# Encoder trunk on one core: shorter GpSimd subtractions, rope casts and a square on other engines, and another order of the first sums

## The chip, the core and the metric

The kernel runs on one core of a Trainium2 chip. The core has a matrix engine (TensorE, PE in the profile; PEld is its loading of weights), three engines for elementwise work (VectorE or DVE, ScalarE or ACT, GpSimd or POOL), and a queue engine (SyncE or SP) from which nearly all transfers start. Each engine takes its instructions in a fixed order, and waits on semaphores for what the others give it. The metric is the time of one execution in microseconds, as the median of several runs. Before the change it is 1354.4 us, the median of three runs from 1353.18 to 1356.97.

## What is computed

Two layers over a sequence of 512 rows of width 1024. Each layer is an attention part and a gated conv-MLP, both scaled and shifted by a vector `c`:

```python
for l in range(DEPTH):
    mod = jax.nn.silu(c) @ w_ada[l] + b_ada[l]
    sh_a, sc_a, gt_a, sh_f, sc_f, gt_f = [m[:, None, :] for m in jnp.split(mod, 6, axis=-1)]
    h = rms_norm(x, g_attn[l]) * (1.0 + sc_a) + sh_a
    x = x + gt_a * hybrid_mixer(h, w_in[l], diff_lambda[l], diff_subln[l], na_rpb[l], w_out[l], l)
    h = rms_norm(x, g_ffn[l]) * (1.0 + sc_f) + sh_f
    x = x + gt_f * conv_glu_ffn(h, w_up[l], conv_w[l], conv_b[l], w_down[l])
return rms_norm(x, g_final)
```

The mixer projects `h` with `w_in` and has three kinds of heads: four differential heads (two softmaxes, the second subtracted with a factor, then a norm over each head), six heads with three dilated windows, and six with a 2-D neighbourhood. The first two kinds turn their queries and keys by rotary angles (rope). The heads' outputs are projected with `w_out`.

## The kernel before

All data lie transposed: eight tiles `x` of 128 features by 512 positions. Products are made from rounded parts: a float32 operand is split into `hi` (rounded to the format fp32r) and `lo` (what is left), and a product is three matmuls, hi by hi, lo by hi and hi by lo (`mm3`, lines 487 to 489; in `v_rows` lines 760 to 762; in `first_g0` line 567).

**Weights** come in 128-partition units in a fixed list `UNITS`: eight units of `w_in` for the first projection ("g0", 768 columns), those of the values ("vd", "vb", "vc"), of the later queries and keys ("b", "cq", "ck", 1024 columns), of the output projection ("o1" with 640 columns, "o2"), and of the MLP. `emit_raw` starts a unit's load on SP (line 333) into one of four buffers `raw` (the first eight units have their own, `graw`). `emit_split` (line 336) makes `hi` by a cast on ACT (line 355) and `lo` by one subtraction over the whole unit (line 357): on POOL for g0 of the first layer, b, cq, ck, vc, vb, o1 and o2 (`on_pool`), on DVE for the rest. There are three buffers for split weights in attention, so a unit is split when an earlier one has been used (`free_unit`).

**Adaptive sums.** `ada_step` (line 406) makes one column of the modulation: a multiply-and-sum over a 512 KB tile of `w_ada` on DVE (line 416, with a short read of the accumulator), for the scales also an instruction on ACT (line 424), and it starts the load of a later tile on SP (`ada_load`, line 403).

**Start.** `first_g0` (line 501) loads `x`, squares its eight tiles on ACT (line 510), adds five of the squares up on DVE (line 512), sums over partitions on PE (line 516), takes the mean on DVE (line 518) and its power on POOL (line 520), spreads it with PE (line 523), multiplies on DVE (line 528), and makes the hi and lo parts of `h` (lines 540 to 543). The first two adaptive sums follow the squares in program order: one scale column and one shift column.

**Attention.** `rope_pair` (line 657) turns one pair of query and key chunks: four products on DVE (lines 669, 670), and for each half a sum (line 676), the cast to `hi` on ACT (line 683) and the `lo` part (line 688); the sum and the `lo` part run on the engine `E`, which is DVE for the pair d0 and POOL for d1, b0, b1 and b2. The four results go to DRAM on SP (line 696), from where the stacked queries and keys come back. A step of the differential heads (`diff_step`, line 992) is: scores on PE (line 1001), a maximum on DVE (line 1003), an exponential on ACT (line 1011), a weighted difference on DVE (lines 1017 to 1019), four transposes on PE (line 909), their `hi` cast on ACT (line 913) and `lo` part on DVE (line 917), and the products with the values on PE (lines 930, 932). `diff_norm` (line 953) norms a pair of heads. Its lines 967 and 968 put together a variance of eight columns on DVE.

**What sets the order.** The program text gives each instruction its place by a counter (`Clock`: a stage of a chain runs some steps after the one before). The framework's planner then fixes the order on each engine ahead of time: among the instructions that are ready by its own estimate it takes the one that was written first, so a later one can overtake an earlier one that isn't ready. On the chip the order is fixed. `tc.issue_after(ins)` ties the instructions of its block that run on `ins`'s engine behind `ins`, and no others.

Of the kernel before, what the change touches and what calls it, by code (L numbers as in the profile page):

```python
# [12 lines left out]
F32 = mybir.dt.float32  # L13
F32R = mybir.dt.float32r
BF16 = mybir.dt.bfloat16
AF = mybir.ActivationFunctionType
ALU = mybir.AluOpType
# [10 lines left out]
EPS = 1e-6  # L28
# [148 lines left out]
def build(ctx, tc, a):  # L177
    nc = tc.nc
    V, A, G, PE, SY = nc.vector, nc.scalar, nc.gpsimd, nc.tensor, nc.sync
# [156 lines left out]
    def emit_split():  # L336
        i = wst["split"]
        l, u = divmod(i, NU)
        kind = UNITS[u][0][0]
        if slots["w"]:  # L340
            w, pool, bufs = "w", wp, W_BUFS
        elif slots["f"] and kind in NEAR:
            w, pool, bufs = "f", fpool["p"], F_BUFS
        else:
            return False
        slots[w] -= 1
        where[i] = w
        wst["split"] += 1
        while wst["raw"] <= i:
            emit_raw()  # L350
        r = raws.pop(i)
        n = r.shape[1]
        hi = pool.tile([128, n], F32R, tag=w + "hi", bufs=bufs, name=f"{w}hi{uid()}")
        lo = pool.tile([128, n], F32R, tag=w + "lo", bufs=bufs, name=f"{w}lo{uid()}")
        A.copy(hi, r)  # L355
        on_pool = (l == 0 and u < 8) or kind in ("b", "cq", "ck", "vc", "vb", "o1", "o2")
        (G if on_pool else V).tensor_tensor(out=lo, in0=r, in1=hi.bitcast(F32), op=ALU.subtract)  # L357
        splits[i] = (hi, lo)
        while wst["auto"] and wst["raw"] < min(TOT, i + RAW_AHEAD):
            emit_raw()  # L360
        return True
# [139 lines left out]
    def first_g0():  # L501
        fp = fpool["p"]
        for _ in range(5):
            ada_load()
            ada_load()
            emit_raw()
        sq = []
        for k in range(KD):
            sq.append(fp.tile([128, S], F32, tag="xt", bufs=8, name=f"xq{k}"))
            A.activation(out=sq[k], in_=x[k], func=AF.Square)  # L510
            if k in (2, 4, 5, 6, 7):
                V.tensor_tensor(out=sq[0], in0=sq[0], in1=sq[k], op=ALU.add)
        st = ps("s", (128, 4))
        todo = [(k, j) for k in (1, 3, 0) for j in range(4)]
        for i, (k, j) in enumerate(todo):
            PE.matmul(st[:, j:j + 1], sq[k][:, j * 128:j * 128 + 128], ones, start=(i == 0), stop=(i == len(todo) - 1))
        v = tmp((128, 4), tag="sm4", bufs=4)
        V.tensor_scalar(out=v, in0=st, scalar1=1.0 / D, scalar2=EPS, op0=ALU.mult, op1=ALU.add)
        r = tmp((128, 4), tag="sm4", bufs=4)
        G.tensor_tensor(out=r, in0=v, in1=mh[:, 0:4], op=ALU.pow)  # L520
        rb = ps("s")
        for j in range(4):
            PE.matmul(rb[:, j * 128:j * 128 + 128], r[:, j:j + 1].to_broadcast([128, 128]), ident, start=True, stop=True)
        xt, h = [], []

        def norm_x(k):
            xt.append(fp.tile([128, S], F32, tag="xt", bufs=8, name=f"xt{k}"))
            V.tensor_tensor(out=xt[k], in0=x[k], in1=rb, op=ALU.mult)

        def mk(k):  # L530
            if wst["raw"] < 8:
                emit_raw()
            t = xt[k]
            emit_split()
            if k >= 1:
                wst["auto"] = True
            sc, sh = gsc[0][:, k:k + 1], mods(0, 0)[:, k:k + 1]
            hi, lo = [wp.tile([128, S], F32R, tag="h", bufs=16, name=f"h{uid()}") for _ in range(2)]
            h.append((hi, lo))
            ins = A.activation(out=hi, in_=t, func=AF.Identity, scale=sc, bias=sh)  # L540
            t2 = tmp()
            A.activation(out=t2, in_=t, func=AF.Identity, scale=sc, bias=sh)
            G.tensor_tensor(out=lo, in0=t2, in1=hi.bitcast(F32), op=ALU.subtract)
            if k == 5:
                with tc.issue_after(ins.ins):
                    late_consts()

        ada_step()
        ada_step()
        norm_x(0)  # L550
        norm_x(1)
        mk(0)
        norm_x(2)
        norm_x(3)
        ada_step()
        ada_step()
        mk(1)
        for k in range(4, KD):
            norm_x(k)
        banks = yield  # L560
        us = {}

        def mms(k, cs):
            wh, wl = us[k]
            for w, m in ((wh, 0), (wl, 0), (wh, 1)):
                for c in cs:
                    PE.matmul(banks[c], w[:, c * 128:c * 128 + 128], h[k][m], start=(k == 0 and w is wh and m == 0),  # L567
                              stop=(k == KD - 1 and m == 1))

        for k in range(KD):  # L570
            if k + 2 < KD:
                ada_step()
                ada_step()
                mk(k + 2)
            us[k] = next_unit(("g0", k))
            if k == 0:
                mms(0, range(5))
            elif k == 1:
                mms(1, range(5))
                mms(0, (5,))  # L580
                mms(1, (5,))
                free_unit()
            else:
                mms(k, range(6))
            if k:
                free_unit()
            ck.step()
        cest.close()
        late["pt"] = ctx.enter_context(tc.tile_pool(name="ppt", bufs=1, space=PSUM))
        yield h  # L590
# [49 lines left out]
    def attention_phase(l, gen, fest):  # L640
# [16 lines left out]
        def rope_pair(name, px, py, tag, ti, eng=None):  # L657
            C, Sn = rope[:, 2 * ti, :], rope[:, 2 * ti + 1, :]
            nv = 4 if name[0] == "d" else 2
            dd = 64 // nv  # L660
            sd = dp.tile([2 * nv, 4 * dd, S], F32, name=f"scr{l}{name[0]}{name[1]}")
            scr[name] = sd
            E = eng or V
            ts, nat = {}, {}

            def part(i):
                def s0():
                    ts[i] = take("tmp"), take("tmp")
                    V.tensor_tensor(out=ts[i][0], in0=(px, py)[i], in1=C, op=ALU.mult)  # L669
                    V.tensor_tensor(out=ts[i][1], in0=(py, px)[i], in1=Sn, op=ALU.mult)  # L670
                    if i == 1:
                        give(tag[0])
                        give(tag[1])

                def s1():
                    E.tensor_tensor(out=ts[i][0], in0=ts[i][0], in1=ts[i][1],
                                    op=(ALU.subtract, ALU.add)[i])
                    give("tmp")

                def s2():  # L680
                    av["nat"] -= 2
                    hi = at([128, S], F32R, "nat", 8)
                    A.copy(hi, ts[i][0])
                    nat[i] = hi

                def s3():
                    lo = at([128, S], F32R, "nat", 8)
                    E.tensor_tensor(out=lo, in0=ts[i][0], in1=nat[i].bitcast(F32), op=ALU.subtract)
                    nat[2 + i] = lo
                    give("tmp")  # L690

                return (0, {"tmp": 2}, s0), (1, {}, s1), (1, {"nat": 2}, s2), (1, {}, s3)

            def s4():
                for c in range(4):
                    SY.dma_start(sd[:, c * dd:c * dd + dd], nat[c].bitcast(F32))
                av["nat"] += 4
                mark(2, ("scr", name))

            ck.chain(*part(0), hold=True)  # L700
            ck.chain(*part(1), (2, {}, s4), hold=True)
# [251 lines left out]
        def diff_norm(c):  # L953
# [7 lines left out]
            def s1():  # L961
                sq = box["sq"]
                st = take("pt", (128, 4, 2))
                for j in range(4):
                    PE.matmul(st[:, j], sq[:, j * 128:j * 128 + 128], blk, start=True, stop=True)
                v = tmp((128, 4, 2), tag="sm8", bufs=6)
                V.scalar_tensor_tensor(out=v, in0=dns[c], scalar=EPS, in1=dns[c], op0=ALU.mult, op1=ALU.mult)
                V.scalar_tensor_tensor(out=v, in0=st, scalar=1.0 / 64, in1=v, op0=ALU.mult, op1=ALU.add)
                give("pt")
                give("tmp")  # L970
                r = tmp((128, 8), tag="sm8", bufs=6)
                G.tensor_tensor(out=r, in0=v.rearrange("p a b -> p (a b)"), in1=mh, op=ALU.pow)
                box["r"] = r
# [405 lines left out]
    out = a["out"].rearrange("m p n -> p m n")  # L1379
# [62 lines left out]
```

## Time and profile before

| | us |
|---|---|
| median of 3 runs | 1354.4 |
| lowest and highest run | 1353.18, 1356.97 |
| the profiled execution | 1349.55 |
| its span, first to last instruction | 1347.8 |
| busy: PE, DVE, ACT, POOL | 1285.7, 849.0, 639.8, 240.0 |

The profile is one execution. Lines are those of the kernel file, a row names the engine, the operation, the tile it writes and those it reads, and busy times are in us. A wait is the idle time of an engine before an instruction, put down to what came last. A stretch is given in us from the start of the span. Layer 0 begins its attention near 58, its MLP near 313; layer 1 near 723 and 970.

### The profile page before, as it was taken

To read this page: it belongs to the slowest core of one execution; us is meant where nothing else is said; L and a number is where in the kernel's file an instruction comes from. 1 tells how busy PE (TensorE), PEld (TensorE's weight loads), DVE (VectorE), ACT (ScalarE), POOL (GpSimd) and SP (SyncE) were. 2 spreads that over 40 slices of the span, in tenths; PEclk is the share of its full clock that TensorE was granted. 3 is DMA by queue.
4 is the path that set the end of the run, shared out by engine and by line. 5 is a ranking of instruction groups with operands and counts; after the bars stand their busy time and mean duration, and the time that the engine had idled before them with its cause. 6 is when DMAs were issued, how large, how long until landed. Compare 5 with 4: busy or idle time off the path is not lost.

```text
span 1347.8 us, 18449 instructions
## 1 busy us (share of the span) xinstructions
PE 1285.7 (95%) x6836; PEld 1102.7 (82%) x6836; DVE 849.0 (63%) x1534; ACT 639.8 (47%) x1150; POOL 240.0 (18%) x163
## 2 busy tenths in 40 slices
PE   5988899899999999999999989999999999999997
PEld 4877698778988888888899868987898888888886
DVE  5659777788676566656674786576775434443443
ACT  4546688665533233323342667887554313331331
POOL 2644522133000000000124344212400000000002
PEclk9999999998999999999999999999999999999999
DMA  9676667853466656665524755472433332333211
GB/s 361 232 207 168 187 199 220 233 161 118 148 204 187 201 175 187 199 191 168 173 77 132 189 156 167 121 212 81 125 118 102 94 94 94 94 94 99 86 36 63
DMA packets 75001, 207.28 MB, mean 154 GB/s; under 512 B 8608, under 2 KB 12576, under 8 KB 74784
## 3 DMA queue, kind: packets, MB, share of 16 engines
q1 hardware_dynamic: 74048, 203.72, 50.4%
q10 hardware_dynamic: 864, 2.39, 0.5%
q8 instruction: 54, 0.88, 0.3%
q14 instruction: 35, 0.29, 0.1%
HBM read 180.91 MB, written 15.73 MB: 146 GB/s over the span
## 4 chain that ended last, share of the span: by engine, by line
PE 72%; DMA 9%; DVE 7%; POOL 4%; issue 4%; ACT 3%; SPq 1%; POOLq 0%; DVEq 0%; ACTq 0%
PE pr L489 9%; PE pr L488 9%; PE pr L487 9%; PE s L488 5%; PE s L487 5%; PE s L489 5%; PE pt L488 4%; PE pt L489 4%; PE pt L487 4%; PE o L488 2%; PE o L489 2%; PE o L487 2%; PE pt L909 2%; DMA raw<-w 1%; PE pr L567 1%
## 5 line engine op out<-in xcount | busy, mean ns | idle before, releaser
L355 ACT CAST whi<-raw 128x1024 fp32r<-128x1024 f32 (+2 forms) x136 | 128.1, 943 | 229.6 <-PE pr L489 78.2
L357 POOL TENSOR_TENSOR wlo<-raw,whi 128x768 fp32r<-128x768 f32 (+2 forms) x58 | 115.0, 1988 | 299.4 <-ACT whi L355 275.4
L448 POOL TENSOR_TENSOR tmp<-tmp,tmp 128x256 f32<-128x256 f32 (+1 forms) x38 | 37.0, 976 | 714.3 <-ACT tmp L446 713.5
L357 DVE TENSOR_TENSOR wlo<-raw,whi 128x1024 fp32r<-128x1024 f32 (+1 forms) x78 | 90.8, 1164 | 101.4 <-ACT whi L355 100.6
L416 DVE CUSTOM_DVE_ANT_0 tmp<-raw,cb,par 128x1024 bf16<-128x1024 f32 x80 | 109.4, 1368 | 52.7 <-DMA raw<-w_ada 52.3
L355 ACT CAST fhi<-raw 128x1024 fp32r<-128x1024 f32 (+1 forms) x76 | 74.6, 985 | 130.6 <-PE pr L489 52.8
L357 DVE TENSOR_TENSOR flo<-raw,fhi 128x1024 fp32r<-128x1024 f32 (+1 forms) x74 | 86.9, 1175 | 56.8 <-ACT fhi L355 56.0
L487 PE MATMUL pr<-h,whi 128*128 128x512 f32 (+1 forms) x300 | 113.2, 378 | 0.4 <-DVE tmp L669 0.4
L489 PE MATMUL pr<-h,whi 128*128 128x512 f32 (+1 forms) x300 | 111.5, 372 | 0.4 <-DVE h L483 0.4
L488 PE MATMUL pr<-h,wlo 128*128 128x512 f32 (+1 forms) x300 | 111.7, 372 | 0.0
L487 PE MATMUL pr<-h,fhi 128*128 128x512 f32 (+1 forms) x244 | 86.8, 358 | 0.1
L488 PE MATMUL pr<-h,flo 128*128 128x512 f32 (+1 forms) x244 | 86.5, 356 | 0.0
L489 PE MATMUL pr<-h,fhi 128*128 128x512 f32 (+1 forms) x244 | 85.8, 358 | 0.3 <-DVE h L483 0.3
L917 DVE TENSOR_TENSOR pl<-pt,ph 128x512 fp32r<-128x512 f32 x80 | 54.6, 685 | 18.0 <-ACT ph L913 17.7
L1267 ACT ACTIVATE tmp<-tmp 128x512 f32<-128x512 f32 x44 | 27.6, 631 | 77.7 <-DVE tmp L1262 77.7
L489 PEld LDWEIGHTS pr<-h,whi 128*128 128x128 f32 x300 | 56.7, 189 | 9.5 <-DVE h L483 0.6
L487 PEld LDWEIGHTS pr<-h,whi 128*128 128x128 f32 x300 | 56.8, 189 | 8.9 <-DVE tmp L669 0.7
L488 PEld LDWEIGHTS pr<-h,wlo 128*128 128x128 f32 x300 | 56.9, 190 | 8.7 <-POOL wlo L357 0.6
L913 ACT CAST ph<-pt 128x512 fp32r<-128x512 f32 x80 | 46.5, 582 | 26.2 <-PE pt L909 25.9
L1003 DVE TENSOR_REDUCE sm<-s 128x1 f32<-128x512 f32 x64 | 42.9, 681 | 25.3 <-PE s L1001 25.0
L909 PE MATMUL pt<-cst,tmp 128*128 128x128 f32 x320 | 48.7, 275 | 9.9 <-DVE tmp L1019 7.0
L909 PEld LDWEIGHTS pt<-cst,tmp 128*128 128x128 f32 x320 | 37.7, 140 | 19.8 <-issue 5.9
(287 smaller groups left out, 3704.9 us busy)
## 6 DMA issues: line engine op xcount, KB each, us to landing
raw<-w SPq DMA_DIRECT2D x132, 512.0 KB
raw<-w_ada SPq DMA_DIRECT2D x80, 512.0 KB
raw<-w SPq DMA_DIRECT2D x64, 384.0 KB
araw<-w_ada SPq DMA_DIRECT2D x16, 512.0 KB
raw<-w SPq DMA_DIRECT2D x16, 320.0 KB
graw<-w SPq DMA_DIRECT2D x8, 384.0 KB
scr0b<-nat SPq DMA_DIRECT2D x12, 256.0 KB
qs<-nat SPq DMA_DIRECT2D x24, 128.0 KB
```

The costliest lines, as they stand in the source:

```text
L355: A.copy(hi, r)
L357: (G if on_pool else V).tensor_tensor(out=lo, in0=r, in1=hi.bitcast(F32), op=ALU.subtract)
L416: V.tensor_tensor_reduce(out=junk, in0=r, in1=cv, op0=ALU.mult, op1=ALU.add, scale=1.0, scalar=par[:, OFF_B + l * 48 + j:OFF_B + l * 48 + ...
L448: self.last = self.eng.tensor_tensor(out=self.sq[0][:, sl], in0=self.sq[0][:, sl], in1=self.sq[m][:, sl], op=ALU.add)
L487: PE.matmul(out, wh, hh, start=first, stop=False)
L488: PE.matmul(out, wl, hh, start=False, stop=False)
L489: return PE.matmul(out, wh, hl, start=False, stop=last)
L909: PE.transpose(pt[:, kt], P[:, kt * 128:kt * 128 + 128], ident)
L913: A.copy(st["ph", half][:, :, sl], pt)
L917: V.tensor_tensor(out=st["pl", half][:, :, sl], in0=st["pt", qb], in1=st["ph", half][:, :, sl].bitcast(F32), op=ALU.subtract)
L1003: V.tensor_reduce(out=nm[:, m:m + 1], in_=s, axis=AX.X, op=ALU.max, negate=True)
L1267: A.activation(out=t, in_=t, func=AF.Silu)
```

## The change

Four edits. The `lo` parts that POOL makes are cut into pieces of 256 columns, one instruction each. In `rope_pair` the cast to `hi` goes to POOL wherever the pair's sums run there. The first adaptive sum is tied behind the last addition of squares. One of the two small DVE instructions in `diff_norm` becomes a square on ACT with the constant inside.

```diff
         A.copy(hi, r)
         on_pool = (l == 0 and u < 8) or kind in ("b", "cq", "ck", "vc", "vb", "o1", "o2")
-        (G if on_pool else V).tensor_tensor(out=lo, in0=r, in1=hi.bitcast(F32), op=ALU.subtract)
+        if on_pool:
+            hf = hi.bitcast(F32)
+            for c in range(0, n, 256):
+                e = min(c + 256, n)
+                G.tensor_tensor(out=lo[:, c:e], in0=r[:, c:e], in1=hf[:, c:e], op=ALU.subtract)
+        else:
+            V.tensor_tensor(out=lo, in0=r, in1=hi.bitcast(F32), op=ALU.subtract)
...
             if k in (2, 4, 5, 6, 7):
-                V.tensor_tensor(out=sq[0], in0=sq[0], in1=sq[k], op=ALU.add)
+                last = V.tensor_tensor(out=sq[0], in0=sq[0], in1=sq[k], op=ALU.add)
...
-        ada_step()
+        with tc.issue_after(last.ins):
+            ada_step()
         ada_step()
...
                     hi = at([128, S], F32R, "nat", 8)
-                    A.copy(hi, ts[i][0])
+                    if E is G:
+                        G.tensor_copy(hi, ts[i][0])
+                    else:
+                        A.copy(hi, ts[i][0])
                     nat[i] = hi
...
-                V.scalar_tensor_tensor(out=v, in0=dns[c], scalar=EPS, in1=dns[c], op0=ALU.mult, op1=ALU.mult)
+                A.activation(out=v, in_=dns[c], func=AF.Square, scale=math.sqrt(EPS))
```

## Rows read from the trace of the kernel before

**Rows 1.** The page's busy table: us, share of the span, instructions.
```profile
PE 1285.7 (95%) x6836; PEld 1102.7 (82%) x6836; DVE 849.0 (63%) x1534; ACT 639.8 (47%) x1150; POOL 240.0 (18%) x163
```

**Rows 2.** By stretch: length, busy time (instructions) of each engine, granted clock, DMA.
```profile
80.00:90.00 10.00, 10.00 (x49) 9.55 (x48) 2.41 (x5) 1.84 (x5) 1.70 (x1) 0.86 0.59 188
...
86.00:166.00 80.00, 69.68 (x371) 56.57 (x370) 69.23 (x134) 51.28 (x113) 33.18 (x17) 1.00 0.69 183
747.00:822.00 75.00, 66.58 (x352) 54.29 (x351) 62.50 (x122) 48.47 (x107) 30.23 (x17) 0.98 0.65 174
```

**Rows 3.** PE's waits, 85 to 170, then 755 to 835: total us, times, longest.
```profile
PE o L930 <- ACT ph L913: 3.6, 3, 2.1
PE pt L909 <- DVE tmp L1019: 3.1, 3, 1.6
...
PE pt L909 <- DVE tmp L1019: 4.0, 3, 2.3
PE o L930 <- ACT ph L913: 2.7, 1, 2.7
```

**Rows 4.** Line 1019 (ns: shortest, median, longest), and single instructions (start, us).
```profile
L1019 DVE SCALAR_TENSOR_TENSOR tmp<-tmp,sm,tmp x32: 731/745/2542, 90.5 to 814.1; 128x512 f32<-128x512 f32 x32
...
104.31 2.23 DVE L1019 SCALAR_TENSOR_TENSOR tmp<-tmp,sm,tmp 128x512 f32<-128x512 f32 x1
...
105.95 2.85 POOL L357 TENSOR_TENSOR wlo<-raw,whi 128x1024 fp32r<-128x1024 f32 x1
...
133.35 0.99 DVE L1019 SCALAR_TENSOR_TENSOR tmp<-tmp,sm,tmp 128x512 f32<-128x512 f32 x1
```

**Rows 5.** ACT's waits for the rope sums, 125 to 170, then 785 to 825.
```profile
ACT nat L683 <- POOL tmp L676: 7.1, 4, 2.7
...
ACT nat L683 <- POOL tmp L676: 8.3, 4, 3.4
```

**Rows 6.** POOL's groups by shape: busy us, mean ns, idle before; line 676's durations.
```profile
L357 POOL TENSOR_TENSOR wlo<-raw,whi 128x1024 fp32r<-128x1024 f32 x20 | 49.0, 2454 | 97.9 <-ACT whi L355 92.8 <-PE pr L762 5.0
L357 POOL TENSOR_TENSOR wlo<-raw,whi 128x768 fp32r<-128x768 f32 x22 | 40.4, 1848 | 99.6 <-ACT whi L355 85.3 <-issue 13.3 <-DMA scr0d<-nat 1.1
...
L448 POOL TENSOR_TENSOR tmp<-tmp,tmp 128x256 f32<-128x256 f32 x28 | 23.0, 824 | 15.1 <-ACT tmp L446 14.2
...
L676 POOL TENSOR_TENSOR tmp<-tmp,tmp x16: 1255/1298/2246, 64.3 to 816.0; 128x512 f32<-128x512 f32 x16
```

**Rows 7.** Instructions in order of time at vb, layer 0, then layer 1.
```profile
72.74 2.52 POOL L688 TENSOR_TENSOR nat<-tmp,nat 128x512 fp32r<-128x512 f32 x2
...
78.18 0.44 PE L761 MATMUL pr<-wlo,h 128*128 128x384 f32 x1 [1.45 <-POOL wlo L357]
...
737.63 1.31 POOL L688 TENSOR_TENSOR nat<-tmp,nat 128x512 fp32r<-128x512 f32 x1
...
740.79 0.44 PE L761 MATMUL pr<-wlo,h 128*128 128x384 f32 x1 [0.20 <-POOL wlo L357]
```

**Rows 8.** The start: a stretch by engine, then instructions in order of time.
```profile
10.00:20.00 10.00, 4.31 (x20) 4.14 (x20) 5.31 (x10) 3.89 (x7) 2.87 (x2) 1.00 1.02 389
...
8.21 3.73 ACT L510 ACTIVATE xq<-x 128x512 f32<-128x512 f32 x7
...
13.46 1.28 DVE L416 CUSTOM_DVE_ANT_0 tmp<-araw,cx,par 128x1024 bf16<-128x1024 f32 x1 [1.56 <-DMA araw<-w_ada]
...
16.47 0.69 DVE L512 TENSOR_TENSOR xq<-xq,xq 128x512 f32<-128x512 f32 x1
...
19.12 0.16 DVE L518 TENSOR_SCALAR sm<-s 128x4 f32<-128x4 f32 x1 [1.96 <-PE s L516]
...
21.87 1.30 SPq L403 DMA_DIRECT2D araw<-w_ada  x2
```

**Rows 9.** Line 967's durations on DVE, and a small instruction on ACT.
```profile
L967 DVE SCALAR_TENSOR_TENSOR sm<-sm x4: 151/156/1701, 116.6 to 818.7; 128x8 f32<-128x8 f32 x4
...
L249 ACT ACTIVATE le<-ls 128x2 f32<-128x2 f32 x2 | 0.3, 196 | 0.0
```

## The prediction

> **What bounds the kernel now.** I read the busy table first: TensorE (PE) is busy 1285.7 us of the span [rows 1], so only some 62 us of idle time can be won by reordering, and no edit here touches a matmul. Next the table by stretch: PE idles 10.3 us of the 80 us from 86 to 166 and 8.4 us of the 75 us from 747 to 822 [rows 2]. These are the stretches, one per layer, in which the attention of the differential heads runs beside projections; VectorE (DVE) is busy there for 69.2 and 62.5 us. Then the waits of PE inside the two stretches [rows 3]: 3.1 + 4.0 = 7.1 us for DVE's L1019 (the weighted difference of the two softmaxes) and 3.6 + 2.7 = 6.3 us for ScalarE's (ACT's) cast L913 of the transposed probabilities. So two late engines explain most of the idle time, and the rows say why each is late.
>
> DVE first. L1019 takes 745 ns as a median but up to 2542 ns [rows 4]. The long ones lie under GpSimd (POOL): the one begun at 104.31 lasts 2.23 us, until 106.5, while a `lo` subtraction of L357 ends and the next begins at 105.95, itself stretched to 2.85 us [rows 4]. Each waits for the whole of the other's instruction, and the turn changes between two POOL instructions that stand back to back. Shorter POOL instructions hold for less: the L1019 at 133.35, beside a 512-column rope instruction, takes 0.99 us [rows 4]. Over all 32, the excess of L1019 over its median is some 9.5 us, by the mean.
>
> ACT next. Its rope casts (L683) stand in ACT's queue ahead of other work and wait for POOL's sum L676: 7.1 us in four waits from 125 to 170 and 8.3 us in four from 785 to 825 [rows 5]. An L913 that PE needs stands behind one of them in each layer.
>
> **The change, part by part.** Every sum below is against the profiled execution, 1349.55 us (span 1347.8); the median of the shown runs is 4.9 us above it, and I add that at the end.
>
> *Pieces of 256 columns.* 68 units have their `lo` part on POOL. The durations lie on a line: 512 columns 1.30 us (L676's median), 768 columns 1.85, 1024 columns 2.45 [rows 6], which puts 256 columns at some 0.73 us with a constant part of about 0.15 us (L448 takes 0.82 on that shape as a mean [rows 6]). A 1024-column unit becomes four pieces, so 0.45 us longer, a 768- or 640-column one 0.3 us longer: 156 further instructions and some 23 us of POOL in all, which is busy for 33.2 of the 80 us of the first stretch [rows 2], so mostly beside other work. The gain: a DVE instruction that meets such a unit waits for at most 0.73 us in place of 2.4. That takes away 1 - 0.73/2.4 = 70% of the 7.1 us that PE waits for L1019: -5.0. Bounds: -7.1 (all of it), and 0, if DVE meets the following pieces with its next instructions. I take the value near the first since L1019 comes only about once per unit, and the instructions between it (reductions from PSUM, L1003) kept their length under POOL. A raw buffer, which the SP queue's next weight load waits for, comes free 0.3 to 0.45 us later; with four of them this costs nothing while loads run ahead, and near the output projection, where they don't, I take +0.5 (0 to +1.5).
>
> *Rope casts on POOL.* In the four rope pairs of a layer that work on POOL (d1, b0, b1, b2) eight casts of 128x512 leave ACT, sixteen in all. ACT's own work falls by 0.62 us each, which is worth nothing by itself. What is worth something is the order: L913 no longer stands behind a wait for POOL. Of the 6.3 us, the largest single wait of each layer (2.1 and 2.7 [rows 3]) is of this kind, so -4 of 4.8, since DVE is late next. Bounds -6.3 and 0. With the stall in the second layer the granted clock's dip after it should shrink; the dip after the stall at 76 shows its price (mean 0.86 over 80 to 90 [rows 2], 1.4 us), of which I take -1.
>
> The price of a cast on POOL is not in the trace. The nearest rows are POOL's two-input instructions on the same shape, near 1.30 us [rows 6]; one input in place of two should lie between half of that and all of it, and I take 0.95. The Trainium skill (GPSIMD Engine Reference, section 4.1 Engine selection) says that one-input work there is roughly at line rate, with 768 ns as a measured figure for 512 elements of a tight loop in section 3.1; by it a cast would be 0.77 and the terms that follow 0.7 us smaller per layer. No run here shows that yet.
>
> What the casts lengthen is POOL's own chain, and behind it in POOL's queue stand the `lo` parts of the second unit of vb. In layer 0 POOL ends the ropes at 72.74 + 2.52 = 75.3 without a gap, and PE's L761 takes up at 78.18 after waiting for it [rows 7]; in layer 1 POOL ends at 738.9 and PE waits 0.20 until 740.79 [rows 7]. Four casts add 3.8 us; PE then needs not the whole unit (1.85) but two pieces (1.46), so layer 0 moves by 75.3 + 3.8 + 1.5 - 78.2 = +2.4 and layer 1 by 738.9 + 3.8 + 1.5 - 740.8 = +3.4, if POOL does the ropes first. If the planner puts the pieces ahead of the casts, nothing moves here, and the rope outputs go out later; their four writes to DRAM (L696) stand on the SP queue with raw weight loads behind them. PE can also take up score matmuls (L1001) in the hole. I take a third of the 5.8: +2 (0 to +8).
>
> Eight of the casts lie in the two stretches and read SBUF as L676 and L688 do, so they can hold DVE. Three of the sixteen POOL rope instructions there hold a DVE one for 0.25 to 0.75 us; half as many again, and mostly shorter, gives +0.5 to +1, and I take +1. The Trainium skill (SBUF — State Buffer, Who interferes with whom) speaks against this edit here: ScalarE never waits for the port that GpSimd and VectorE share. By that rule each cast is a new hold of its full length, in the worst case 8 x 0.95 = 7.6 us in place of my +1.
>
> *First sums.* The last addition of squares starts at 16.47, behind two adaptive sums (L416, 1.28 us, the first of them from 13.46) [rows 8], though the squares are done at 11.9 [rows 8]. The edit ties only the first of the two behind it, and only its instructions on DVE; its scale on ACT follows the sum anyway, and the load that it issues on SP goes out at 21.87 [rows 8], some 4 us after the sum would end. The planner that preferred a sum to an addition will do so with the second one, whose load lands near 14.8: one transfer (512 KB at 389 GB/s [rows 8], 1.3 us) after the first, for which DVE waited until 13.46. Then 14.8 + 1.2 + 0.6 = 16.6 is the end of the additions in place of 17.1: -0.5. Bounds: 0, and -3.1 (both sums behind the additions and done at 16.0, where L518 now runs at 19.1 [rows 8]).
>
> *Square on ACT.* Four times a DVE instruction of 156 ns (one held up to 1701) gives way to one on ACT of some 0.2 us [rows 9]. It waits for nothing that its DVE successor does not wait for, so 0; the bounds are -1.5 (the held one was on DVE's path) and +0.5.
>
> **Sum:** -5.0 + 0.5 - 4 - 1 + 2 + 1 - 0.5 + 0 = -7.0, so 1342.5 for an execution like the profiled one, and 1354.4 - 7.0 = 1347.4 for the median.
>
> **Rivals.** (1) *POOL's queue becomes the gate of vb* (slower than before). A cast at 1.30 makes the chain 5.2 us longer: layer 0 moves by 3.8 and layer 1 by 4.8; a second dip of the clock like the one after 76 adds 1.4, the holds of the casts 1 to 2, while the gains above come in by half (-4 to -5): +6, so 1360. It decides from the point where POOL's first two pieces of the second vb unit land over 3 us later than now and PE has no other matmul ready. For it: POOL ran those ropes with no gap, and PE already stalls there in layer 0. Against it: the pieces let the planner start PE sooner. (2) *The waits only change hands* (no change): DVE meets one piece after the other, or the chain waits next for something that was as late, such as L917 behind L913. Then holds and order give 2 or 3 us together, against some 3 on the other side: 1354. Against it stands the turn that changed at 105.95. (3) *Both adaptive sums go behind the squares*: the start gains 3.1 in place of 0.5, and the projection behind it carries that on: 1344.8. Against it: nothing ties the second sum.
>
> **How the numbers follow.** A measurement of this kernel tells about 0.3%, or 4.1 us, from no change (the runs shown spread over 3.8). The forecast, 1347.4, gets 0.55; rival 1 gets 0.17, rival 2 0.18, rival 3 0.10. Range: all gains at their ends, with rival 3, give -7.1 - 6.3 - 1 - 3.1 = -17.5, so 1337; at the other end rival 1 begins near 1357. I give 1337 to 1358, which leaves out most of rival 1. Faster: the forecast without its weakest part, 0.53, and rival 3, 0.63 in all. Slower: 0.17. Within: 0.20.
>
> **What would show each step.** Right: the longest L1019 falls from 2.5 to about 1.5 us and PE's waits for it to about 2 us; ACT has no wait for L676 left, and PE's waits for L913 fall under 2.5; POOL has 224 `lo` instructions near 0.75 us and 16 casts under 1 us; the last addition of squares starts near 16.0. Wrong: PE waits over 2 us for L357 at vb in both layers; L1019's mean stays near 1.0 us; the stretch from 86 to 166 keeps its 10 us of idle PE; or a weight load waits on SP behind L696.

## The result, and the profile after

The changed kernel takes 1337.46 us (median of 4 runs, 1331.26 to 1340.21), the kernel before in the same session 1355.66 (4 runs, 1353.18 to 1356.97). The ratio is 0.9868, 95% interval 0.9837 to 0.9900: faster, by 17.9 us, with 13.6 to 22.1 in the interval. The profiled execution took 1335.26 us (span 1333.5), 14.3 less than the one before. Of all the runs below one, of the kernel l16, took 1574.4 us at a granted clock of 0.84 where the others have 0.98 or more, and the numbers leave it out. In the changed file the lines stand lower: 357 is now 361, 416 is 422, 518 is 524, 676 is 683, 761 is 771, 909 is 919, 913 is 923, 1019 is 1029, 1036 is 1046; the cast on POOL is line 691. New here are line 1050, which adds the mask to the dilated heads' scores and takes the minimum of each row on DVE, line 927, the `lo` part of the transposed probabilities (917 before), line 940, their product with the values (930 before), and line 1088, the scores of the neighbourhood heads (1078 before).

The busy table and, under it, two stretches of the changed kernel (length, then busy us and instructions of PE, PEld, DVE, ACT, POOL, the granted clock, DMA share, GB/s), beside [rows 1] and [rows 2]:
```profile
PE 1280.6 (96%) x6836; PEld 1100.7 (83%) x6836; DVE 835.5 (63%) x1530; ACT 631.4 (47%) x1138; POOL 283.7 (21%) x335
...
86.00:166.00 80.00, 72.77 (x384) 59.09 (x383) 68.40 (x140) 52.11 (x114) 45.36 (x48) 0.99 0.69 183
747.00:822.00 75.00, 74.28 (x417) 62.65 (x416) 64.42 (x139) 56.99 (x127) 43.62 (x49) 1.00 0.63 172
```
PE's idle time in the span falls from 62.1 to 52.9 us, and it is busy 5.1 us less for the same 6836 matmuls; why it is busy less is not shown. The second stretch is now full: PE idles 0.7 us of 75, where it idled 8.4. The first still idles 7.2 of 80.

PE's waits of the changed kernel, from 60 to 175 and from 715 to 835 (us in total, times, longest), and the lines of the weighted difference (shortest, median and longest in ns; then its group with busy us and mean ns), beside [rows 3] and [rows 4]:
```profile
PE s L1046 <- DVE sm L1050: 4.9, 1, 4.9
PE pr L771 <- POOL wlo L361: 3.7, 1, 3.7
PE pt L919 <- DVE pl L927: 1.6, 2, 1.3
PE o L940 <- ACT ph L923: 0.7, 1, 0.7
...
PE pr L771 <- POOL wlo L361: 2.4, 1, 2.4
PE pt L919 <- DVE tmp L1029: 0.4, 1, 0.4
...
L1029 DVE SCALAR_TENSOR_TENSOR tmp<-tmp,sm,tmp x32: 730/744/1605, 87.1 to 804.6; 128x512 f32<-128x512 f32 x32
...
L1029 DVE SCALAR_TENSOR_TENSOR tmp<-tmp,sm,tmp 128x512 f32<-128x512 f32 x32 | 25.9, 811 | 0.3
```
Both waits that the change was aimed at are nearly gone: 7.1 us for L1019 have become 0.4, 6.3 for L913 have become 0.7. Two others are there instead: 6.1 us for POOL's `lo` parts at vb (1.45 and 0.20 before, [rows 7]), and 4.9 us for L1050 in layer 0.

POOL's groups by shape in the changed kernel (busy us, mean ns), and the casts' own durations, beside [rows 6]:
```profile
L361 POOL TENSOR_TENSOR wlo<-raw,whi 128x256 fp32r<-128x256 f32 x178 | 136.2, 795 | 257.9 <-ACT whi L355 234.1 <-issue 12.6 <-DMA ks<-nat 7.7
L361 POOL TENSOR_TENSOR wlo<-raw,whi 128x128 fp32r<-128x128 f32 x16 | 7.4, 462 | 0.0
...
L691 POOL CAST nat<-tmp x16: 606/614/1115, 62.7 to 807.8; 128x512 fp32r<-128x512 f32 x16
```
A cast takes 614 ns, less than half of the 1298 of a two-input instruction on that shape [rows 6].

The start of the changed kernel in order of time (start us, duration), beside [rows 8]:
```profile
10.39 3.08 DVE L518 TENSOR_TENSOR xq<-xq,xq 128x512 f32<-128x512 f32 x4 [0.35 <-ACT xq L516]
13.48 1.28 DVE L422 CUSTOM_DVE_ANT_0 tmp<-araw,cx,par 128x1024 bf16<-128x1024 f32 x1
...
15.43 0.16 DVE L524 TENSOR_SCALAR sm<-s 128x4 f32<-128x4 f32 x1 [0.66 <-PE s L522]
15.51 1.27 DVE L422 CUSTOM_DVE_ANT_0 tmp<-araw,cx,par 128x1024 bf16<-128x1024 f32 x1
```
The additions run without a break and end at 13.5, where the last of them used to start at 16.47. The mean runs at 15.43 and no longer at 19.12, since the planner put the second adaptive sum behind it. PE's first projection starts at 20.5 in place of 24.2.

Where the time came in, by the first or last start of a line in the two profiled executions: in layer 0 the first projection is 3.7 us early, the first scores of the dilated heads (line 1046) 9.5, the first scores behind them (line 1088) only 4.6, and the second part of the output projection (line 1219) 3.1. In layer 1 the rope products (line 676) are 3.8 us early, the first scores of the differential heads (line 1011), behind the wait at vb, 0.3 late, their last 8.8 early, and the last output projection (line 898) 12.5. So layer 0 keeps nothing of its shorter stretch, and most of the gain comes in in layer 1. The drop from 9.5 to 4.6 is a new hole in layer 0, in four places of the trace in order of time:
```profile
156.06 0.61 SPq L740 DMA_DIRECT2D ql<-scr0b  x1
156.77 0.54 SPq L409 DMA_DIRECT2D raw<-w_ada  x1
...
162.58 1.28 DVE L422 CUSTOM_DVE_ANT_0 tmp<-raw,cb,par 128x1024 bf16<-128x1024 f32 x1 [6.29 <-DMA raw<-w_ada]
...
164.54 0.80 PE L1046 MATMUL s<-ks,qs 128*128 128x512 f32 x1 [4.85 <-DVE sm L1050]
```
An adaptive sum heads DVE's queue and waits 6.3 us for its weights. Their load left SP at 156.77, behind the loads of the dilated heads' stack (their stacked queries and keys). L1050 stands behind the sum on DVE, and PE's next scores wait for L1050; from 160 to 170 PE is busy 5.46 us at a granted clock of 0.83.

### The profile page after: what moved, and what is told of

It reads as the page before. It is cut to its first block, busy times and chain, and to the rows that moved or that the text cites. A ratio compares the mean times of both kernels' runs of the same rounds, so it can differ in the third digit from the quotient of the medians.

```text
span 1333.5 us, 18622 instructions
## 1 busy us (share of the span) xinstructions
PE 1280.6 (96%) x6836; PEld 1100.7 (83%) x6836; DVE 835.5 (63%) x1530; ACT 631.4 (47%) x1138; POOL 283.7 (21%) x335
## 3 DMA queue, kind: packets, MB, share of 16 engines
q10 hardware_dynamic: 864, 2.39, 0.5%
## 4 chain that ended last, share of the span: by engine, by line
PE 77%; DVE 7%; DMA 5%; issue 4%; ACT 3%; POOL 3%; SPq 1%; POOLq 0%; DVEq 0%; ACTq 0%
PE pr L495 10%; PE pr L493 10%; PE pr L494 10%; PE s L494 5%; PE s L493 5%; PE s L495 5%; PE pt L494 4%; PE pt L495 4%; PE pt L493 4%; PE o L495 2%; PE o L494 2%; PE o L493 2%; PE pt L919 2%; DMA raw<-w_ada 1%; PE pr L574 1%
## 5 line engine op out<-in xcount | busy, mean ns | idle before, releaser
L361 POOL TENSOR_TENSOR wlo<-raw,whi 128x256 fp32r<-128x256 f32 (+1 forms) x194 | 142.9, 768 | 257.9 <-ACT whi L355 234.1
L1021 ACT ACTIVATE tmp<-s,sm 128x512 f32<-128x512 f32 x64 | 43.8, 692 | 22.7 <-DVE sm L1013 19.4
L493 PE MATMUL pr<-oh,whi 128*128 128x512 f32 (+1 forms) x128 | 49.6, 387 | 2.9 <-ACT oh L1160 2.9
```

The costliest lines, as they stand in the source:

```text
L361: G.tensor_tensor(out=lo[:, c:e], in0=r[:, c:e], in1=hf[:, c:e], op=ALU.subtract)
L493: PE.matmul(out, wh, hh, start=first, stop=False)
L1021: A.activation(out=Ps[m], in_=ss[m], func=AF.Exp, bias=nm[:, m:m + 1], accum_out=dn if m else ld)
```

## The experiments

**One edit at a time.** Each part alone on the kernel before, in one session (before: 1353.66, 29 runs):
```diff
s_pieces:  +  for c in range(0, n, 256): G.tensor_tensor(out=lo[:, c:e], ...)
s_casts:   +  if E is G: G.tensor_copy(hi, ts[i][0])
s_sums:    +  with tc.issue_after(last.ins): ada_step()
s_square:  +  A.activation(out=v, in_=dns[c], func=AF.Square, scale=math.sqrt(EPS))
```
Pieces. 

> Before plus the pieces of 256 columns alone. Theory A (the holds of VectorE by whole-unit subtractions are what the pieces remove): the mean of the weighted difference falls from 1040 to under 850 ns, PE's waits for it from 7.1 to under 3 us, the median falls by 5 to 8 us. Rival B (the waits only change hands): the mean falls but PE's idle time in the two stretches stays over 15 us in sum, and the median falls by less than 2 us.

Casts. 

> Before plus the rope casts on GpSimd alone. Theory A (ScalarE no longer stands behind GpSimd's sums): PE's waits for the cast of the transposed probabilities fall from 6.3 to under 3 us, the median falls by 3 to 5 us net of a longer stall at the value projection (+2). Rival B (the stall at the value projection eats it): PE waits over 5 us there in sum and the median changes by less than 2 us or rises.

Sums. 

> Before plus the tied first sum alone. Theory A (the start gains what the profile of the changed kernel shows there, and the layers carry it on): the last addition of squares ends near 13.5 instead of 17.1, PE's first projection matmul starts 3.5 us earlier, and the median falls by 3 to 4 us. Rival B (the DVE-bound stretch of layer 0 or a weight load swallows it): the start gains 3.5 us, the median less than 1.5. Rival C (the plan made new for all that follows outweighs the start): a change of more than 6 us either way.

Square. 

> Before plus the square on ScalarE alone. Theory A: the one held instruction of 1.7 us goes, the median falls by 0 to 1.5 us, within what can be told from no change. Rival B (an instruction more on ScalarE's queue in the DVE-bound stretch delays exponentials): up to +1 us.

| alone | median us (runs) | ratio, interval | gain us | forecast |
|---|---|---|---|---|
| pieces | 1345.40 (6) | 0.9940, 0.9918 to 0.9962 | 8.3 | 4.5 |
| casts | 1350.19 (12) | 0.9980, 0.9961 to 0.9998 | 3.5 | 2.0 |
| sums | 1350.72 (12) | 0.9979, 0.9962 to 0.9996 | 2.9 | 0.5 |
| square | 1351.28 (12) | 0.9980, 0.9964 to 0.9995 | 2.4 | 0 |

The gains are differences of the medians and add up to 17.1; the change as a whole has 18.2 by that reckoning. The last three intervals begin near no change: they leave 0.3 to 5.3 us for the casts, 0.5 to 5.1 for the sums and 0.7 to 4.9 for the square. So the sums' theory A (3 to 4) and rival B (under 1.5) are not told apart by the time, nor is it shown that the square gives more than theory A's 1.5. With the sums alone the first projection starts 3.3 us early and the first scores of the dilated heads 1.6. The profiled executions of these two kernels, 1352.74 and 1352.88, are longer than the one before (1349.55), so they do not show where their gains came in.

In the kernel with the pieces alone, the group of the weighted difference (busy us, mean ns), and PE's waits from 86 to 175 and from 715 to 835:
```profile
L1025 DVE SCALAR_TENSOR_TENSOR tmp<-tmp,sm,tmp 128x512 f32<-128x512 f32 x32 | 27.0, 845 | 0.2
...
PE o L936 <- ACT ph L919: 3.7, 3, 2.0
...
PE pt L915 <- DVE tmp L1025: 0.8, 2, 0.5
...
PE o L936 <- ACT ph L919: 3.4, 2, 3.2
```
The pieces take PE's waits for DVE from 7.1 to 1.2 us and leave those for ACT's cast (6.3 before, 7.1 now): the two late engines of the prediction are two separate waits. DVE is busy 836.4 us in place of 849.0, with as many instructions. Not all of the 5.9 us come out as time. These are the two stretches of [rows 2] with the pieces alone:
```profile
86.00:166.00 80.00, 72.03 (x365) 58.02 (x364) 65.88 (x133) 51.82 (x113) 38.77 (x42) 0.96 0.70 192
747.00:822.00 75.00, 67.57 (x360) 55.12 (x359) 59.60 (x128) 50.43 (x111) 33.92 (x37) 0.98 0.67 171
```
PE idles 15.4 us in them where it idled 18.7, and 57.8 in the whole span where it idled 62.1. Over 15 us was rival B's sign, so half of rival B was there, though the time fell by four times its 2 us. Waits for the stacked queries and keys (1.0 and 2.0 us) have come in. From the first differential to the first dilated scores the two layers take 66.3 and 63.3 us (65.5 and 63.7 before), with the casts alone 64.1 and 59.8, and in the changed kernel 59.5 and 54.6. In these single executions most of the shortening comes only when both waits are gone.

Another part comes in ahead of the stretches: the first differential scores start 2.7 us sooner, 2.4 of it from 58 to 87, where the granted clock is 1.00 in place of 0.94. The kernel with the square alone, whose edit first runs after that stretch, has 1.00 there too and is 1.3 us early at those scores, so how much of this is due to the pieces is not shown.

In the kernel with casts alone, PE's waits from 60 to 175 and from 715 to 835, and an adaptive sum on DVE:
```profile
PE pr L764 <- POOL wlo L357: 4.7, 1, 4.7
PE s L1039 <- DVE sm L1043: 3.5, 1, 3.5
PE pt L912 <- DVE tmp L1022: 3.1, 3, 1.6
...
PE o L933 <- ACT ph L916: 0.7, 1, 0.7
...
PE pt L912 <- DVE tmp L1022: 4.3, 4, 2.3
PE pr L764 <- POOL wlo L357: 2.6, 1, 2.6
...
171.33 1.28 DVE L416 CUSTOM_DVE_ANT_0 tmp<-raw,cb,par 128x1024 bf16<-128x1024 f32 x1 [4.76 <-DMA raw<-w_ada]
```
The reverse: the wait for ACT falls from 6.3 to 0.7, that for DVE stays (7.4), and the wait at vb grows to 7.3, over the 5 us that rival B named. That is 5.6 us gained and 5.7 given back. And the hole of the changed kernel is there already: the dilated heads' scores wait 3.5 us for line 1043 (1050 in the changed file), behind an adaptive sum that waits for its load. The traces before and with the pieces, the sums or the square alone have no such wait of PE. Over the span PE idles 62.0 us, as before (62.1), and the profiled execution is only 1.7 us below the one before. So by the traces the casts win and lose the same in waits, and where the 3.5 us of the medians come from was not settled.

**Pieces of other widths** in the changed kernel (these and the runs of the next paragraph in one session, before 1352.60, 11 runs):
```diff
-            for c in range(0, n, 256):
-                e = min(c + 256, n)
+            for c in range(0, n, 512):      # w512; 128 in w128
+                e = min(c + 512, n)
```


> The changed kernel with GpSimd's lo parts in pieces of 512 columns instead of 256 (one such instruction took 1.26 us in the kernel before, a piece of 256 columns 0.80). Theory (a DVE instruction that shares its moment with GpSimd is held for what is left of GpSimd's instruction): the longest multiply of the softmax by its sums lies near 1.9 us, its mean between the 811 ns of 256 columns and the 1040 of whole tiles, some 870, and the time is up by a third to a half of the 8.2 us that the pieces gave alone: 1340 to 1342. Rival (only the count of GpSimd's instructions matters, and 512 columns have less of it): the mean stays near 810 and the time is 1335 to 1338.

> The changed kernel with GpSimd's lo parts in pieces of 128 columns (462 ns for one in the changed kernel, 3.7 us for 1024 columns against 3.2 in pieces of 256). Theory (the hold is as long as GpSimd's instruction): the mean of the softmax's multiply falls to some 770 ns from 811 and its longest to 1.2 us, worth under 1 us, while the wait at vb grows by 0.5 us for each row of weights behind which TensorE stands, 2 to 4 us in both layers together: 1338 to 1342. Rival (the holds still cost most): 1333 to 1336.

With 512 columns 1337.74 us (ratio 0.9886, 0.9868 to 0.9904), with 128 columns 1342.06 (0.9914, 0.9896 to 0.9933); 256 columns have 0.9868 (0.9837 to 0.9900). The line of the weighted difference (shortest, median and longest in ns) and groups with busy us and mean ns, 512 columns:
```profile
L1029 DVE SCALAR_TENSOR_TENSOR tmp<-tmp,sm,tmp x32: 731/741/1739, 87.4 to 806.0; 128x512 f32<-128x512 f32 x32
...
L1029 DVE SCALAR_TENSOR_TENSOR tmp<-tmp,sm,tmp 128x512 f32<-128x512 f32 x32 | 28.4, 888 | 0.3
...
L361 POOL TENSOR_TENSOR wlo<-raw,whi 128x512 fp32r<-128x512 f32 x78 | 103.1, 1333 | 274.4 <-ACT whi L355 251.8 <-issue 13.1 <-PE pr L772 4.9
```
and 128 columns:
```profile
L1029 DVE SCALAR_TENSOR_TENSOR tmp<-tmp,sm,tmp x32: 734/748/1187, 89.1 to 805.2; 128x512 f32<-128x512 f32 x32
...
L1029 DVE SCALAR_TENSOR_TENSOR tmp<-tmp,sm,tmp 128x512 f32<-128x512 f32 x32 | 25.9, 811 | 0.2
...
L361 POOL TENSOR_TENSOR wlo<-raw,whi 128x128 fp32r<-128x128 f32 x372 | 172.4, 499 | 233.4 <-ACT whi L355 193.1 <-PE pt L919 17.7 <-issue 12.0
```
The longest weighted difference follows the length of POOL's instruction: 2424 to 2722 ns in the four kernels with whole units, 1739 with 512 columns, 1301 to 1605 in the eight with 256, 1187 with 128, near the 1.9 and 1.2 us expected for 512 and 128. The mean falls from 1040 over 888 (870 expected) to 811 and does not fall further at 128. A mean of one trace is not that sharp: the four kernels with whole units have 901 to 1053, the eight with 256 columns 804 to 856.

For 512 columns the theory held in its rows, but not in the time, which stays within the interval of the changed kernel, where the rival had put it. For 128 columns the fall of the mean to 770 did not come, and neither did a longer wait at vb: 3.2 and 3.0 us, where it is 3.7 and 2.4 with 256. The time is 4.3 us above that with 512 in the same session, at the upper edge of what was expected, but not for the reason given, and the two intervals overlap by a little. Its six executions go with the granted clock: 1336.96 and 1338.62 at 0.989 and 0.988, the other four 1341.77 to 1343.54 at 0.986 to 0.981. The profiled execution is the fastest of the six and does not show what lowers the clock in the others, so that stays open.

**The casts, all or half of them taken back** in the changed kernel:
```diff
-                    if E is G:
+                    if name[0] == "b" and name[1]:     # l_casts; u_casts: A.copy for all
                         G.tensor_copy(hi, ts[i][0])
```


> The changed kernel, with only the casts of the rotated tiles of the second and third pairs of the dilated heads on GpSimd (8 of the 16); those of the second differential pair and of the first dilated pair, which lie just ahead of the vb weights in GpSimd's queue, are back on ScalarE. Theory (the stall at vb is a real cost): TensorE's wait for the weights' lo parts at vb, 3.7 and 2.4 us in the changed kernel, falls to at most 1.5 in each layer, its wait for ScalarE's ph stays under 1.5, and the time is 1337.5 less some 3 to 4.5, about 1333.5. Rival (the wait changes hands): the lo wait falls, but TensorE waits as long for a rope tile, a probability or the load of the masks, and the time is 1336 to 1339.

> The changed kernel with all 16 casts back on ScalarE (the other three edits stay). Theory (the casts free ScalarE ahead of the dilated heads' probabilities, and pay part of that back at vb): TensorE's wait for ScalarE's ph at the dilated heads comes back, 2.5 to 3.7 us in each layer instead of 0.7 and less, the wait for the lo parts at vb falls from 3.7 and 2.4 to 1.5 and less, and the time is 1337.5 plus the 3.4 that the casts gave alone, about 1341. Rival (the two waits cancel): 1336 to 1339.

With half of the casts, 1336.36 us (ratio 0.9877, 0.9856 to 0.9898): no difference to the changed kernel that these intervals show. Its waits of PE, 60 to 175 and 715 to 835:
```profile
PE s L1046 <- DVE sm L1050: 5.4, 1, 5.4
PE s L1011 <- DMA qs<-scr0d: 1.7, 1, 1.7
PE pr L493 <- ACT whi L355: 1.5, 1, 1.5
PE pr L771 <- POOL wlo L361: 1.1, 1, 1.1
...
PE s L1011 <- DMA qs<-scr1d: 1.5, 1, 1.5
```
The wait at vb falls from 3.7 and 2.4 us to 1.1 and none, and PE then waits for the stacked queries of the differential heads and for a weight's `hi` part. The first differential scores come 2.0 and 4.9 us sooner than in the changed kernel, and the first dilated ones 1.9 later and 1.3 sooner, so that nearly all of it is lost again within the stretch. The rival held: the stall at vb is real, and in these traces nearly nothing comes of removing it, since the next thing was as late. The times alone would still leave room for a gain of 3 to 4 us. Without any cast on POOL, 1340.04 (0.9902, 0.9885 to 0.9918), as the theory said (1341). PE's waits there, in the same two stretches:
```profile
PE o L937 <- ACT ph L920: 3.6, 3, 1.9
...
PE pr L768 <- POOL wlo L361: 1.0, 1, 1.0
...
PE o L937 <- ACT ph L920: 3.2, 1, 3.2
```
That is 3.7 us above the kernel with half of them in the same session, though the intervals overlap: in the company of the other edits the casts seem to give what they give alone, and the half on the pairs b1 and b2 all of it. PE's wait of 4.9 us for line 1050 is gone without the casts. So here too the waits balance: over the span PE idles 52.8 us, in the changed kernel 52.9, and it is busy 4.4 us more, for which the trace shows no reason.

**The square taken back** in the changed kernel (before 1354.42, 11 runs):
```diff
-                A.activation(out=v, in_=dns[c], func=AF.Square, scale=math.sqrt(EPS))
+                V.scalar_tensor_tensor(out=v, in0=dns[c], scalar=EPS, in1=dns[c], op0=ALU.mult, op1=ALU.mult)
```


> The changed kernel with the square of the dilated heads' sums back on DVE (four instructions of 128x8; the other three edits stay). Theory (taken alone the square gave 2.4 us because one of its four on DVE was held for 1.7 us behind a whole lo part of GpSimd; with pieces of 256 columns the hold is gone): none of the four takes more than 1.2 us, and the time is that of the changed kernel, 1336 to 1339. Rival (the place in DVE's queue is what pays, whatever the hold): 1339 to 1341.

1335.90 us (ratio 0.9857, 0.9833 to 0.9881), and the four instructions back on DVE (ns):
```profile
L977 DVE SCALAR_TENSOR_TENSOR sm<-sm x4: 288/494/731, 117.0 to 810.4; 128x8 f32<-128x8 f32 x4
```
None is held for more than 0.73 us, where one was held for 1.70 before [rows 9]. The theory held: with the pieces in place no gain of the square is seen, though the intervals of the two ratios leave room for the 2.4 us that it gave alone. Two things differ in the trace of the square alone: the held instruction is gone, and the mean of the weighted difference is 901 ns with the same long `lo` units. Whether either of them made the 2.4 us was not tried.

**Taking the new hole away.** In layer 0, from step 10 on, one more load of adaptive weights is issued ahead of a stack of the attention, where fewer than two are already in hand:
```diff
             if stacks and stacks[0][0] in ready and si >= stacks[0][1]:
+                if l == 0 and si >= 10 and ada_st["n"] < 39 and len(ada_raw) < 2:
+                    ada_load()
                 stacks.pop(0)[2]()
```
on the changed kernel (ap4) and on the one with half of the casts (lp4). A third kernel (l16, half of the casts) instead starts the adaptive sums of the attention later, with `si >= 16` in place of `si >= 10`. All three in one session, before 1353.61 (11 runs):

> The changed kernel, in which ahead of each stack of the attention the load of one more row of adaptive weights is issued, so that the adaptive sum in layer 0 whose load stands behind the dilated heads' stack on SP has it already. Theory (the wait of DVE for that load, 6.3 us, and of TensorE for DVE behind it, 4.9 us, is time given back): no wait of TensorE for the sm of the dilated heads over 1 us near 160, the granted clock of 160 to 170 back above 0.95, and the time 4 to 5 us under the changed kernel's: about 1333. Rival (the dilated heads' own transfers, issued in the same microseconds, or a weight that now finds no raw buffer, are next): 1336 to 1340.

> The kernel with 8 casts on GpSimd, and with the same earlier load of adaptive weights. Theory (with the wait at vb and the wait for the adaptive load both gone, nothing near them takes their place): 1336.4 less 4 to 5, about 1332, the fastest of all. Rival (the casts on ScalarE and the loads meet the same transfers): 1335 to 1339.

> The kernel with 8 casts on GpSimd, whose adaptive sums in the attention of layer 0 begin with step 16 of its list instead of step 10, after the first stacks of the dilated heads; three more sums are left for the stretch behind the attention. Theory (a sum that stands behind its load in DVE's queue holds the dilated heads' probabilities up): the wait of TensorE for sm near 160, 5.4 us with the sums from step 10, is under 1.5, and the time about 1332. Rival (the second of the moved sums still waits for a load behind the second stack, or the three left over cost DVE 4 us where TensorE waits for it): 1335 to 1339.

The earlier load gives 1329.03 us on the changed kernel (6 runs, 1325.90 to 1336.69; ratio 0.9820, 0.9792 to 0.9849) and 1332.62 with half of the casts (0.9849, 0.9816 to 0.9881). The second time is the one expected, but that kernel is not the fastest of all, as had been expected too. The later sums give 1336.76 (five runs; 0.9871, 0.9844 to 0.9899), nothing. The first kernel's PE waits from 140 to 180, all of them, and two stretches as above:
```profile
PE pt L919 <- DVE pl L927: 1.8, 1, 1.8
...
86.00:166.00 80.00, 76.86 (x418) 62.72 (x417) 73.22 (x152) 57.67 (x125) 47.77 (x49) 1.00 0.68 188
160.00:170.00 10.00, 10.00 (x61) 8.77 (x60) 4.76 (x13) 7.11 (x15) 3.38 (x4) 1.00 0.78 259
```
The 4.9 us are gone and the clock stays at 1.00. By the first starts, the scores of line 1088 come 4.6 us earlier than in the changed kernel, as the theory had it. The output projection behind them comes 8.3 us earlier: a second wait of PE in the changed kernel, 5.5 us at line 1088 for which the profile names no releaser, is gone too, and 3.3 us for a `lo` part on DVE stand in its place. This second gain was not foreseen. Of all versions this is the fastest; against the changed kernel the intervals of the ratios overlap by a little (0.9837 to 0.9849), so that it beats the changed kernel is likely, not certain.

In l16 the wait for L1050 is gone as well (no wait of PE over 1.5 us from 140 to 180), yet the time did not move. The stretch behind the attention, from 296 to 400, says why; first the kernel with half of the casts, whose sums run earlier (columns as above):
```profile
296.00:400.00 104.00, 101.82 (x639) 92.06 (x638) 81.70 (x138) 50.01 (x76) 15.58 (x16) 0.99 0.53 164
```
and l16:
```profile
296.00:400.00 104.00, 97.29 (x592) 88.07 (x591) 76.30 (x132) 47.15 (x74) 10.89 (x13) 0.95 0.52 163
```
PE is busy 4.5 us less there, and at 0.95 of its clock. The second part of the output projection (line 1219) still begins 4.5 us sooner in l16, at 292.1, so the gain is given back behind it. The three sums left over stand there, where the MLP begins, as the rival had it; that they are what costs the time was not tried by itself.

## Why the prediction was right, and where it was not

The forecast was faster, by 7.0 us, and it is faster, by 17.9; 1337.46 lies at the lower end of the range, half a microsecond inside it. That end was the sum of all gains at their bounds, so that the range held is in part luck. The waits that were named are the ones that went. But nearly every size was too small, and a wait was taken for time too readily.

- **Pieces** (-5.0 + 0.5 forecast, -8.3 alone). The hold was read rightly: the longest L1029 is 1605 ns (some 1.5 us forecast), PE waits 0.4 us for it (2), and the longest follows the width of the piece. The step that failed is the one from waits to time: the term took 70% of the waits for L1019 as time. The pieces took 83% of them (7.1 to 1.2), but PE's idle time fell by only 4.3 us, and in the profiled execution with the pieces alone the way from the first differential to the first dilated scores is as long as before (66.3 and 63.3 us for 65.5 and 63.7). 2.4 us came in between 58 and 87, where [rows 3] don't look, and are not surely theirs. So the 8.3 us are only in part where the term put them, and the place of the rest is open. The `lo` parts became 224 instructions, as forecast, with a median of 0.74 to 0.79 us; they cost POOL 32.9 us with the pieces alone, where 23 were reckoned.
- **Casts, ACT's side** (-4 - 1). PE's waits for L913 fell by 5.6 us, and ACT waits for no rope sum of the pairs on POOL any more. As waiting, the term was right within 1.6.
- **Casts, POOL's side** (+2 of 5.8). The price of a cast was taken as 0.95 us and is 0.61. The planner did the ropes first, as the full term assumed, and the sign that I had named as proof of error was there: PE waits 3.7 and 2.4 us for `lo` parts at vb. By the first differential scores behind vb the two layers lost 0.2 and 4.1 us of their lead there. Rival 1's mechanism took place, with +4.5 us of waiting, and did not decide: with most of the wait removed (half of the casts) the time is the same within what the runs tell. What failed here is the sign of being wrong: a wait over 2 us was named as a loss without asking what PE would have waited for next. One price was left out altogether, the hole in layer 0: PE's wait for L1050 is 3.5 us with the casts alone and 4.1 to 5.5 in the changed kernel and its variants with other pieces, half of the casts or the square taken back, and it is in no trace without the casts. The net of all this is 3.5 us alone, against 2.0 forecast.
- **The casts' holds on DVE** (+1). The Trainium skill (SBUF — State Buffer, Who interferes with whom) has GpSimd and VectorE lock each other out of a shared port, ScalarE never. In the rows the hold runs both ways: a cast at 126.16 takes 0.96 us beside an L1029 that takes 0.99, and the 16 casts have a mean of 744 ns over a median of 614, so that they are themselves held for 2.1 us in all. With the casts alone DVE is busy 850.2 us where it was 849.0, with the same 1534 instructions, so the term had about the right size.
- **First sums** (-0.5). This is the step that failed most. I wrote that the planner would put the second sum ahead of an addition, as it had with the first, for its load lands in time. In the trace the second sum stands behind the additions and even behind the mean, although only the first is tied. The mean moved by 3.7 us, more than my outer bound of 3.1: with nothing between them the additions ended at 13.5 and the mean ran at 15.43, where I had put 16.0. Rival 3, given 0.10, is what happened. Alone the edit gave 2.9 us.
- **Square** (0). Not refuted in the company of the pieces (the kernel without it is no slower). Alone the median gives 2.4, beyond the bound of -1.5, but its interval reaches down to 0.7; what it came from was not shown.
- **The sum.** The parts alone add up to 17.1 us. Of the 10.1 above the forecast, 3.8 are the pieces, 2.4 each the sums and the square, 1.5 the casts. Since no gain of the square is seen beside the pieces, some 2 us of the whole, within its interval, are not assigned to a part.

## What to carry to other kernels

When two engines hold each other up for the length of an instruction, cut the long one to about the length of the short one: from whole units over 512 to 256 columns the longest hold fell, and 128 columns lowered the mean no further. In the time, 512 and 256 columns were not told apart. A wait in a trace, old or new, has a price only if nothing as late stands behind it, so test it by removing it before counting it as a gain or a loss. Here 5.9 us less waiting for DVE took 4.3 us off PE's idle time, removing 5.0 of the 6.1 us at vb brought nothing that the runs show, and one load held in hand earlier was worth some 6, by the ratios (3.8 with half of the casts, intervals overlapping in both). When a planner fixes the order, ask of a tie not only what is tied, but what else becomes ready in the gap that the tie opens.

## What was not expected of the hardware

A cast of 128x512 on POOL takes 614 ns against 1298 for a two-input instruction on the same shape. The Trainium skill (GPSIMD Engine Reference, section 4.1 Engine selection) calls one-input work there roughly line rate, and the trace agrees: the same cast took 621 ns on ACT before the change. The 769 ns that its section 3.1 measured for 512 elements of a tight loop is more than the 614 of the median cast here.

POOL's instructions are held by DVE as well. A `lo` piece of 256 columns takes 750 ns as a mean at the start (x24, from `graw`) and 795 in the attention. Around 126 us of the changed kernel, POOL's instructions and then DVE's:
```profile
124.80 1.29 POOL L683 TENSOR_TENSOR tmp<-tmp,tmp 128x512 f32<-128x512 f32 x1
126.16 0.96 POOL L691 CAST nat<-tmp 128x512 fp32r<-128x512 f32 x1
...
128.44 2.28 POOL L683 TENSOR_TENSOR tmp<-tmp,tmp 128x512 f32<-128x512 f32 x1
...
125.66 0.99 DVE L1029 SCALAR_TENSOR_TENSOR tmp<-tmp,sm,tmp 128x512 f32<-128x512 f32 x1
...
127.17 2.39 DVE L422 CUSTOM_DVE_ANT_0 tmp<-raw,cb,par 128x1024 bf16<-128x1024 f32 x1
```
The cast and the weighted difference stretch each other by 0.3 us. The adaptive sum takes 2.39 us in place of 1.28, and the rope sum that begins within it 2.28 in place of 1.29.
